# ConvGLU FFN by Strassen-Winograd on one core: two of four weight sums and the residual sums made by accumulating DMAs, the other sums moved to VectorE

## The chip, the cores and the metric

The kernel runs on one core of a Trainium2 chip. The metric is the device time of one execution in microseconds (us), taken as the median of several runs. A core has a matrix engine (PE, with PEld for its weight loads), VectorE (DVE), ScalarE (ACT), GpSimd (POOL) and SyncE (SP). SP issues the plain DMAs in order, POOL issues the DMAs that its own queue carries, and every engine works through its own instructions in the order in which the program has them.

## The reference

One layer: `x += W_out [GDN | FoX | RG-LRU](norm(x))`, then `x += ConvGLU(norm(x))`, then a final RMSNorm, for 512 prompt tokens and 8 streams of 16 tokens (640 tokens together), model width 2048, FFN width 5632, all in float32. The part that the change touches is

```
def conv_ffn(h, conv_past, w_up, conv_w, w_down):
    gp, val = jnp.split(h @ w_up, 2, axis=-1)
    gc, conv_new = causal_conv(gp, conv_past, conv_w)
    return (jax.nn.silu(gc) * val) @ w_down, conv_new
```

## The kernel before, in words

Tokens lie in the free dimension, features on the 128 partitions. A float32 product is made of three float32r products: a weight is split into a high part `wh` (a cast on ACT) and a low part `wl` (a subtraction on DVE), the activations likewise, and PE adds high times high, high times low and low times high in PSUM.

The first 1.2 ms hold the input projection, the mixers and the output projection. Then comes the FFN, with Winograd's form of Strassen's scheme: a matrix product of 2 by 2 blocks (halves of K, pairs of feature tiles, halves of 320 tokens) is done with seven block products instead of eight. The weights of one step arrive as a tile `w` of four 128x128 blocks A21, A11, A12, A22 (256 KB). I call such a tile **a weight**. Four sums S1 to S4 of its blocks are needed, and the seven operands A11, A12, A22, S1 to S4 are split into `wh` and `wl`. PE runs 21 matmuls of 320 columns for one weight (line 1077), in order, into seven PSUM tiles `p`, of which there are eight.

- `wino_w` (lines 1034 to 1055) does this for a weight: SP loads `w` (line 1042); POOL makes S1, S2 and S4 (lines 1047, 1049, 1052), DVE S3 (1048); ACT casts twice (1050 for three blocks, 1053 for four), DVE subtracts twice (1051 and 1054). `w` has 4 buffers, `wh` and `wl` 3 each. `next_w` (1057) keeps three weights ahead.
- `wino_x` (1009 to 1032) makes the seven operands of a pair of activation tiles: four subtractions on POOL (1013 to 1016), three casts on ACT, three subtractions on DVE (1025, 1028, 1031).
- `up(f)` (1331) is one up **pass**: 8 weights, then the combination of the seven products into a gate tile and a value tile (lines 1346 to 1353: one copy on ACT, nine operations on DVE), a multiplication by `corr` on POOL (1354), the convolution (line 257, twice on DVE), silu on ACT (1358), a second multiplication by `corr` on POOL (1359), four products on DVE (1362, 1366), and a store of the result to DRAM (`hT`, 1367) that POOL issues. There are 44 passes, 352 weights.
- `down(i)` (1396) is one down pass: 2 to 8 weights for one of eight pairs of output tiles. It loads the residual tiles from DRAM (`x2`, line 1402, SP), adds the seven products to them (1412, 1418, 1419 on DVE; 1415 on POOL), and stores them (1430, SP). Each pair is visited four times, 32 passes and 168 weights, the first eight passes 2, 3, 3, 4, 5, 6, 7 and 8 weights long. `form` (1377) prepares the operands of the next steps between two weights.
- `plain` (1442) and `finish` (1469) do the last step without Strassen's scheme and the final norm.

The code is written as generators, and a scheduling layer decides how the instructions stand on each engine; the sums and splits of later weights are interleaved with the work that follows a pass.

Of the kernel before, what the change touches and what calls it, by code (L numbers as in the profile page):

```python
# [35 lines left out]
def blk(t, b):  # L36
    """Token block b of a tile in halves order: 4 prompt blocks, then the samples."""
    if b < 4:
        c = (b // 2) * HALF + (b % 2) * 128
        return t[:, c:c + 128]  # L40
    return t.rearrange("p (a c) -> p a c", a=2)[:, :, 256:320]


def cblk(t, b):
    """Token block b of a tile in conv order (prompt, then per stream 3 columns apart)."""
    if b < 4:
        return t[:, 128 * b:128 * b + 128]
    return t[:, 515:667].rearrange("p (s c) -> p s c", c=19)[:, :, :16]


class K:
    def __init__(self, ctx, tc, a, cfg):
# [18 lines left out]
        # the activation tables load beside the first transfers  # L71
# [33 lines left out]
    def rsqrt(self, x, scale, eps, n, out=None):  # L105
        """(x * scale + eps) ** -0.5 to float32's accuracy."""
# [65 lines left out]
    def ahead(self, n):  # L172
        """the next pieces' two parts, up to n of them"""
# [6 lines left out]
    def split_act(self, x, g, hi, lo):  # L180
        """hi + lo = x * g exactly, for each k tile."""
# [17 lines left out]
    def bcast_tok(self, r, name):  # L199
        """r [128 tokens, 5] -> [128, 640]: r's columns one after the other, on each partition."""  # L200
# [12 lines left out]
    def evac(self, out, ps, scale=None):  # L213
        """halves order"""
# [8 lines left out]
    def evac_nat(self, out, ps, np_=P):  # L223
        """prompt tokens in order, then the samples' tokens"""
# [23 lines left out]
    def conv(self, out, x, w, width, bias=None):  # L248
        """out[c] = sum_j w[j] x[c + j] (+ bias)"""
# [11 lines left out]
    def load_x(self):  # L261
        """x * g in two parts; and the sums of x squared; yields k tile by k tile"""
# [7 lines left out]
        # the first two feature tiles' weights between the tiles of x: the second one's at half the pace  # L270
# [11 lines left out]
        # the sums of squares run behind: the odd tiles' on Pool, the even ones' on ACT and DVE  # L282
# [26 lines left out]
    def gates(self, ps):  # L309
        """softplus-based gates of GDN and FoX, their running sums, in the forms that the mixers use"""  # L310
# [16 lines left out]
        # softplus(z), token-major: z (16 columns per token block), -lambda of the LRU (4 columns)  # L327
# [44 lines left out]
        # the caches' log forget values: their sums  # L372
# [15 lines left out]
        # chunk sums of the GDN gates, running sums of the FoX ones  # L388
# [7 lines left out]
        # token-major: beta and G of the heads  # L396
# [8 lines left out]
        # exp(G), -beta exp(G), beta / 2  # L405
# [6 lines left out]
        # G of the last token of its chunk, for each token  # L412
# [11 lines left out]
        # the FoX sums as three bfloat16 parts  # L424
# [17 lines left out]
    def parts3(self, outs, x, tmp):  # L442
        """outs: three bfloat16 parts whose sum is -x"""
# [8 lines left out]
    def gdn_in(self, h, f0):  # L452
        """projections and convolutions of head h: 2 silu(.) of q, k, v, and of z"""
# [31 lines left out]
    def gdn(self, h, y, zs):  # L485
# [6 lines left out]
        # token-major, normalised, and back  # L492
# [22 lines left out]
        # decays  # L515
# [33 lines left out]
        # M, then A^T  # L549
# [19 lines left out]
        # (I + M)^-1 by doubling blocks: X the inverse, Z its transpose  # L569
# [51 lines left out]
        # the prompt's chunks, one after the other  # L621
# [35 lines left out]
        # the samples: their 8 states, each against its 16 columns of 32  # L657
# [42 lines left out]
        # norm, gate  # L700
# [8 lines left out]
    def from_blocks(self, f, out, pt, other):  # L709
        """f on pieces of (out, blocks order pt, other), out and other in halves order"""  # L710
# [5 lines left out]
    def head_norm(self, o, scale=1.0):  # L716
        """o [128 tokens, 5 blocks, 128]: over each block's columns"""
# [17 lines left out]
    def pad32(self, x):  # L735
        """[128, 8 streams x 16] -> [128, 8, 32]: stream s at its half of 32 columns, zeros beside it"""
# [1004 lines left out]
```

## Time and profile before

| | before |
|---|---|
| median of 3 runs | 3004.94 us (3001.29 to 3005.12) |
| span of the profiled execution, first to last instruction | 3000.6 us |
| mean granted TensorE clock in it | 0.983 |
| PE busy | 2888.2 us (96%) |
| DVE busy | 2315.5 us (77%) |
| POOL busy | 1631.7 us (54%) |
| ACT busy | 1109.7 us (37%) |

The profiled execution is told by its span; its own time as a run is not told apart, but it can't be under the span, and the three runs begin 0.7 us above it. The page has, for the 40 equal slices of the span (75 us each), the busy tenths of each engine and the granted clock. A group line names source line, engine, operation and tiles, and ends with the busy time, the mean of one, and the idle time of that engine just before. Timeline rows begin with the start in us from the span's start and the duration.

### The profile page before, as it was taken

Reading aid. Unit: us, or ns where it says so; the run is one execution under the profiler, and the core shown is the slowest. Engines: PE = TensorE matmul, PEld = TensorE weight load, DVE = VectorE, ACT = ScalarE, POOL = GpSimd, SP = SyncE. Lnnn points to the kernel's source line nnn. Section 1 sums busy time; section 2 is a strip of 40 time slices with the busy share of each in tenths; the row PEclk is TensorE's granted clock in tenths of the full one; section 3 lists DMA queues with packets and bytes.
Section 4 is the critical chain, followed back from the end, with each engine's and each line's share of the span. In section 5 each row is a group of like instructions: output and inputs, shape, how many; then the busy total and the mean of one; then the engine's idle time right before and its main releaser. Section 6 shows DMA issues by size and latency. Waiting matters only on the chain. (4 is left out here: it accounts for less than half of the span.)

```text
span 3000.6 us, 54322 instructions
## 1 busy us (share of the span) xinstructions
PE 2888.2 (96%) x19927; PEld 2804.4 (93%) x19927; DVE 2315.5 (77%) x3976; ACT 1109.7 (37%) x2023; POOL 1631.7 (54%) x2367
## 2 busy tenths in 40 slices
PE   8999999999999999999999999999999789999997
PEld 7999999999999999999999999999999789999996
DVE  8746545645634537899999999999999988999888
ACT  4333323323322313444444443444444334434433
POOL 3312200310300014677777777777777988888775
PEclk9999999999999999999999999999999899999998
DMA  5123143134134745433333333333333555555443
GB/s 207 56 93 109 59 143 121 59 123 143 58 109 150 264 130 179 130 105 98 98 99 101 98 98 103 99 101 98 98 98 98 171 160 156 164 163 173 155 138 119
DMA packets 175772, 369.68 MB, mean 123 GB/s; under 512 B 20137, under 2 KB 25145, under 8 KB 175505
## 3 DMA queue, kind: packets, MB, share of 16 engines
q1 hardware_dynamic: 169088, 340.28, 36.4%
q0 software_dynamic: 6416, 25.94, 2.4%
q8 instruction: 156, 2.56, 0.4%
q14 instruction: 112, 0.91, 0.1%
HBM read 306.75 MB, written 59.39 MB: 122 GB/s over the span
## 5 line engine op out<-in xcount | busy, mean ns | idle before, releaser
L1077 PE MATMUL p<-x,wh 128*128 128x320 f32 x7280 | 1625.0, 312 | 45.0 <-DVE t L1412 31.9
L1077 PEld LDWEIGHTS p<-x,wh 128*128 128x128 f32 x7280 | 1230.5, 190 | 56.4 <-DVE t L1412 36.2
L1077 PE MATMUL p<-x,wl 128*128 128x320 f32 x3640 | 1138.9, 313 | 8.9 <-DVE wl L1054 5.2
L1077 PEld LDWEIGHTS p<-x,wl 128*128 128x128 f32 x3640 | 691.5, 190 | 19.9 <-DVE wl L1054 15.1
L1054 DVE TENSOR_TENSOR wl<-ws,wh 128x512 fp32r<-128x512 f32 x520 | 527.4, 1014 | 25.3 <-ACT wh L1053 25.2
L1051 DVE TENSOR_TENSOR wl<-w,wh 128x384 fp32r<-128x384 f32 x520 | 449.6, 865 | 73.4 <-ACT wh L1050 67.7
L1053 ACT CAST wh<-ws 128x512 fp32r<-128x512 f32 x520 | 321.6, 619 | 389.4 <-POOL ws L1052 340.1
L146 PE MATMUL d<-xh,whi 128*128 128x320 f32 x1536 | 396.8, 327 | 0.0
L1050 ACT CAST wh<-w 128x384 fp32r<-128x384 f32 x520 | 264.8, 509 | 330.0 <-issue 169.8
L1052 POOL TENSOR_TENSOR ws<-w,ws 128x128 f32<-128x128 f32 x520 | 352.7, 678 | 40.4
L146 PE MATMUL d<-xl,whi 128*128 128x320 f32 x1536 | 370.8, 310 | 0.0
L146 PE MATMUL d<-xh,wlo 128*128 128x320 f32 x1536 | 370.5, 310 | 0.0
L1047 POOL TENSOR_TENSOR ws<-w 128x128 f32<-128x128 f32 x520 | 284.1, 546 | 150.3 <-DVE wl L1054 144.0
L1049 POOL TENSOR_TENSOR ws<-ws,w 128x128 f32<-128x128 f32 x520 | 344.0, 662 | 37.5
L135 DVE TENSOR_TENSOR wlo<-raw,whi 128x512 fp32r<-128x512 f32 x230 | 175.1, 761 | 212.5 <-ACT whi L134 204.8
L134 ACT CAST whi<-raw 128x512 fp32r<-128x512 f32 x230 | 142.4, 619 | 405.9 <-PE d L146 354.1
L146 PEld LDWEIGHTS d<-xh,whi 128*128 128x128 f32 x1536 | 256.9, 190 | 9.5 <-issue 5.5
L146 PEld LDWEIGHTS d<-xl,whi 128*128 128x128 f32 x1536 | 262.6, 189 | 0.2 <-issue 0.2
L146 PEld LDWEIGHTS d<-xh,wlo 128*128 128x128 f32 x1536 | 262.7, 189 | 0.0
L1048 DVE TENSOR_TENSOR ws<-w 128x128 f32<-128x128 f32 x520 | 218.3, 426 | 13.2 <-DMA w<-in_w_down 0.7
L868 POOL COPY q<-t 128x128 f32<-128x128 f32 x24 | 12.1, 523 | 261.2 <-DVE t L220 139.8
L257 DVE SCALAR_TENSOR_TENSOR t<-t,prm,t 128x656 f32<-128x656 f32 (+1 forms) x136 | 138.4, 1017 | 6.5 <-ACT t L253 3.5
(395 smaller groups left out, 3513.5 us busy)
## 6 DMA issues: line engine op xcount, KB each, us to landing
w<-in_w_up SPq DMA_DIRECT2D x352, 256.0 KB, 2.6
raw<-in_w_in SPq DMA_DIRECT2D x196, 256.0 KB, 2.8
w<-in_w_down SPq DMA_DIRECT2D x184, 256.0 KB, 2.7
t<-x SPq DMA_DIRECT2D x74, 320.0 KB, 3.6
kc<-in_ckT SPq DMA_DIRECT2D x32, 512.0 KB, 5.0
vc<-in_cv SPq DMA_DIRECT2D x32, 512.0 KB, 5.8
x<-t SPq DMA_DIRECT2D x48, 320.0 KB, 2.2
hT<-t POOLq DMA_DIRECT2D x44, 320.0 KB, 2.5
```

The source lines that it names most:

```text
L134: nc.scalar.copy(hi[:, :n], raw[:, :n])
L135: nc.vector.tensor_sub(lo[:, :n], raw[:, :n], hi[:, :n].bitcast(F32))
L146: self.nc.tensor.matmul(ps[h][:, :HALF], wt[:, w], x[:, h * HALF:(h + 1) * HALF], start=start and i == 0, stop=stop and i == 2)
L1047: nc.gpsimd.tensor_add(s[:, 0], w[:, 0], w[:, 3])
L1048: nc.vector.tensor_sub(s[:, 2], w[:, 1], w[:, 0])
L1049: nc.gpsimd.tensor_sub(s[:, 1], s[:, 0], w[:, 1])
L1050: nc.scalar.copy(hi[:, 0:3], w[:, 1:4])
L1051: nc.vector.tensor_sub(lo[:, 0:3], w[:, 1:4], hi[:, 0:3].bitcast(F32))
L1052: nc.gpsimd.tensor_sub(s[:, 3], w[:, 2], s[:, 1])
L1053: nc.scalar.copy(hi[:, 3:7], s)
L1054: nc.vector.tensor_sub(lo[:, 3:7], s, hi[:, 3:7].bitcast(F32))
L1077: nc.tensor.matmul(ps[p], l[:, wi], r[:, xi], start=i == 0 and j == 0, stop=i == n - 1 and j == 2)
```

## The change

Only the FFN is touched (besides comments). Signs and order of the blocks are changed so that the sums come out in place:

- `w` becomes a tile of seven blocks with 6 buffers, `ws` is gone. `wino_raw` loads it with two DMAs of SP (line 1045: two blocks, 128 KB; line 1046: three blocks, 192 KB), and then a DMA of POOL (line 1047) adds a fourth block, read twice, to the two blocks that line 1045 loaded: two of the four sums. It waits for line 1045's data.
- `wino_w` makes the other two sums on DVE, one after the other in place (lines 1055 and 1056, 128x128 each), and casts all seven blocks on ACT at once (1060). `wino_lo` subtracts all seven at once on DVE (1065, 128x896). `next_raw` keeps up to five loaded weights.
- `wino_x` works on a tile of seven blocks (2 buffers instead of 3), with three subtractions on DVE (1020, one of double width, 1021, 1022) and two splits.
- `combine` is shared by up and down: one copy on ACT (1112) and seven results on DVE (nine instructions in `up`, whose gate is written in two pieces). The two multiplications by `corr` in `up` are on DVE (1386, 1391).
- `down` no longer loads the residual nor adds to it. It makes the products' sums in fresh tiles, and two DMAs of POOL (line 1445) add these to `x2` in DRAM; in the last eight passes POOL's DMAs (1443) add `x2` to the tiles in SBUF instead.
- `ns_fc` is loaded by four DMAs instead of one, and the program's space for POOL's DMA descriptors is set to 4096.

```
-        nc.sync.dma_start(w.rearrange("p a c -> p (a c)"), src)
-        nc.gpsimd.tensor_add(s[:, 0], w[:, 0], w[:, 3])
-        nc.vector.tensor_sub(s[:, 2], w[:, 1], w[:, 0])
-        nc.gpsimd.tensor_sub(s[:, 1], s[:, 0], w[:, 1])
-        nc.scalar.copy(hi[:, 0:3], w[:, 1:4])
-        nc.vector.tensor_sub(lo[:, 0:3], w[:, 1:4], hi[:, 0:3].bitcast(F32))
-        nc.gpsimd.tensor_sub(s[:, 3], w[:, 2], s[:, 1])
-        nc.scalar.copy(hi[:, 3:7], s)
-        nc.vector.tensor_sub(lo[:, 3:7], s, hi[:, 3:7].bitcast(F32))
+    def wino_raw(self, src, plain):
+        w = self.wf.tile([P, 7, P], F32, tag="w", bufs=6, name=self.name("w"))
...
+            nc.sync.dma_start(w[:, 3:5], src[:, 2:4])
+            nc.sync.dma_start(w[:, 0:3], src[:, 1:4])
+            nc.gpsimd.dma_start(w[:, 3:5], src[:, 0:1].to_broadcast([P, 2, P]), accum_op=OP.add)
+    def wino_w(self, w, plain):
...
+            nc.vector.tensor_add(w[:, 5], w[:, 3], w[:, 2])
+            nc.vector.tensor_add(w[:, 6], w[:, 0], w[:, 5])
...
+        nc.scalar.copy(hi[:, 0:n], part)
+    def wino_lo(self, part, hi, lo):
...
+        self.nc.vector.tensor_sub(lo[:, 0:n], part, hi[:, 0:n].bitcast(F32))
+    def next_raw(self):
+        while len(self.wr) <= 4:
...
-        nc.gpsimd.tensor_sub(t[:, 0], f[:, 1], f[:, 0])
-        nc.gpsimd.tensor_sub(t[:, 1], f[:, 3], t[:, 0])
-        nc.gpsimd.tensor_sub(t[:, 2], f[:, 3], f[:, 1])
-        nc.gpsimd.tensor_sub(f[:, 1], f[:, 2], t[:, 1])
+        nc.vector.tensor_tensor(f[:, 4:6], f[:, 3:4].to_broadcast([P, 2, HALF]), f[:, 1:3], op=OP.subtract)
+        nc.vector.tensor_sub(f[:, 6], f[:, 1], f[:, 5])
+        nc.vector.tensor_sub(f[:, 3], f[:, 0], f[:, 6])
...
-            nc.gpsimd.tensor_mul(x[:, 2:], x[:, 2:], corr[:, 2:])
+            nc.vector.tensor_mul(x[:, 2:], x[:, 2:], corr[:, 2:])
...
-            nc.gpsimd.tensor_mul(y[:, :656], y[:, :656], corr[:, 2:])
+            nc.vector.tensor_mul(y[:, :656], y[:, :656], corr[:, 2:])
...
+                if last:
+                    nc.gpsimd.dma_start(y[e], x2[2 * i + e], accum_op=OP.add)
+                else:
+                    nc.gpsimd.dma_start(x2[2 * i + e], y[e], accum_op=OP.add)
...
+    nc = _bacc.Bacc("TRN2", target_bir_lowering=False, num_devices=1, dynamic_dma_scratch_size=4096)
```

How the instructions stand now is decided by the scheduling layer. Three places matter. In the rows, `w` is a weight, `wh` and `wl` its parts, `ws` its sums, `p` a PSUM tile, `f` and `x` an operand before and after its split, `t` a work tile; the numbers tell tiles apart.

DVE before, the last weights of an up pass ahead of its combination:

```order
L1048 TENSOR_TENSOR ws_3220_21770<-w_3219_21769 128x128
L1051 TENSOR_TENSOR wl_3218_21738<-w_3215_21735,wh_3217_21737 128x384
L1054 TENSOR_TENSOR wl_3218_21738<-ws_3216_21736,wh_3217_21737 128x512
L1048 TENSOR_TENSOR ws_3224_21804<-w_3223_21803 128x128
L1051 TENSOR_TENSOR wl_3222_21772<-w_3219_21769,wh_3221_21771 128x384
L1054 TENSOR_TENSOR wl_3222_21772<-ws_3220_21770,wh_3221_21771 128x512
```

DVE now, at the same place (the pass ends with weight w_2996; after the last row comes its combination):

```order
L1055 TENSOR_TENSOR w_3005_21239<-w_3005_21239 128x128
L1056 TENSOR_TENSOR w_3005_21239<-w_3005_21239 128x128
L1055 TENSOR_TENSOR w_3008_21270<-w_3008_21270 128x128
L1056 TENSOR_TENSOR w_3008_21270<-w_3008_21270 128x128
L1065 TENSOR_TENSOR wl_3010_21277<-w_2996_21146,wh_3009_21276 128x896
L1055 TENSOR_TENSOR w_3011_21301<-w_3011_21301 128x128
L1056 TENSOR_TENSOR w_3011_21301<-w_3011_21301 128x128
L1065 TENSOR_TENSOR wl_3013_21308<-w_2999_21177,wh_3012_21307 128x896
L1055 TENSOR_TENSOR w_3014_21332<-w_3014_21332 128x128
L1065 TENSOR_TENSOR wl_3016_21339<-w_3002_21208,wh_3015_21338 128x896
```

The weights follow each other as w_2996, 2999, 3002, 3005, 3008, 3011, 3014. Before, a sum (1048) stands one weight ahead of the split that follows it; now the sum (1055) of w_3008 stands ahead of the split (1065) of w_2996, four weights earlier, that of w_3011 ahead of the split of w_2999, and that of w_3014 ahead of the split of w_3002. Over the passes the distance goes 4, 4, 4, 3, 2, 2, 2, 3.

POOL before, around the store of a pass's result:

```order
L1049 TENSOR_TENSOR ws_3166_21361<-ws_3166_21361,w_3165_21360 128x128
L1052 TENSOR_TENSOR ws_3166_21361<-w_3165_21360,ws_3166_21361 128x128
L1367 DMA hT_12549<-t_3145_21225 128x640
L1047 TENSOR_TENSOR ws_3170_21395<-w_3169_21394 128x128
L1049 TENSOR_TENSOR ws_3170_21395<-ws_3170_21395,w_3169_21394 128x128
```

POOL now:

```order
L1047 DMA w_2999_21177<-in_w_up 128x2x128
L1047 DMA w_3002_21208<-in_w_up 128x2x128
L1399 DMA hT_12534<-t_2988_21113 128x640
L1047 DMA w_3005_21239<-in_w_up 128x2x128
L1047 DMA w_3008_21270<-in_w_up 128x2x128
L1047 DMA w_3011_21301<-in_w_up 128x2x128
```

In place of three sums for each weight POOL has one DMA for each, and the store stands between them.

DVE before, in a down pass:

```order
L1048 TENSOR_TENSOR ws_4306_29198<-w_4305_29197 128x128
L1048 TENSOR_TENSOR ws_4310_29234<-w_4309_29233 128x128
L1025 TENSOR_TENSOR x_4304_29194<-f_4279_29057,x_4303_29193 128x640
L1051 TENSOR_TENSOR wl_4308_29200<-w_4305_29197,wh_4307_29199 128x384
L1054 TENSOR_TENSOR wl_4308_29200<-ws_4306_29198,wh_4307_29199 128x512
```

DVE now, in a down pass (weights w_3894, 3897, 3900, 3903, 3906, 3920, 3925, 3928):

```order
L1055 TENSOR_TENSOR w_3920_28180<-w_3920_28180 128x128
L1065 TENSOR_TENSOR wl_3922_28187<-w_3897_28028,wh_3921_28186 128x896
L1032 TENSOR_TENSOR x_3924_28212<-f_3909_28154,x_3923_28211 128x960
L1032 TENSOR_TENSOR x_3924_28212<-f_3909_28154,x_3923_28211 128x1280
L1065 TENSOR_TENSOR wl_3927_28221<-w_3900_28060,wh_3926_28220 128x896
L1056 TENSOR_TENSOR w_3920_28180<-w_3920_28180 128x128
L1055 TENSOR_TENSOR w_3925_28214<-w_3925_28214 128x128
L1056 TENSOR_TENSOR w_3925_28214<-w_3925_28214 128x128
L1055 TENSOR_TENSOR w_3928_28246<-w_3928_28246 128x128
L1056 TENSOR_TENSOR w_3928_28246<-w_3928_28246 128x128
L1065 TENSOR_TENSOR wl_3930_28253<-w_3903_28092,wh_3929_28252 128x896
```

Here too the sum of a weight stands ahead of the split of the weight four before it, at every second split: w_3920 ahead of w_3897, w_3928 ahead of w_3903.

More of the change, by code (lines that the diff above doesn't have):

```diff
@@ L1040, in wino_w @@
+    def wino_w(self, w, plain):
+        nc = self.nc
+        part = w[:, 0:4] if plain else w
+        if not plain:
+            nc.vector.tensor_add(w[:, 5], w[:, 3], w[:, 2])
+            nc.vector.tensor_add(w[:, 6], w[:, 0], w[:, 5])
         hi = self.wf.tile([P, 7, P], F32R, tag="wh", bufs=3, name=self.name("wh"))
         lo = self.wf.tile([P, 7, P], F32R, tag="wl", bufs=3, name=self.name("wl"))
-        nc.sync.dma_start(w.rearrange("p a c -> p (a c)"), src)
-        if plain:
-            nc.scalar.copy(hi[:, 0:4], w)
-            nc.vector.tensor_sub(lo[:, 0:4], w, hi[:, 0:4].bitcast(F32))
-            return hi, lo
@@ L1047, in wino_w @@
[L1047 to L1054 removed]
+        n = part.shape[1]
+        nc.scalar.copy(hi[:, 0:n], part)
@@ L1061, in next_w @@
                 break
-            self.wq.append(self.wino_w(*src))
+            self.wr.append(self.wino_raw(*src))
+        return self.wr.pop(0) if self.wr else None
+    def next_w(self):
+        while len(self.wq) < 3:
+            if self.wn is None:
+                raw = self.next_raw()
+                self.wn = raw and self.wino_w(*raw)
+            if self.wn is None:
+                break
+            now, raw = self.wn, self.next_raw()
+            self.wn = raw and self.wino_w(*raw)
+            self.wq.append(self.wino_lo(*now))
         return self.wq.pop(0)
@@ L1082, in wino, with combine @@
         return ps
+    def combine(self, ps, u, c11, c12, c21, c22):
+        nc = self.nc
+        u1, u2 = u
+        nc.scalar.copy(u1, ps[1])
+        nc.vector.tensor_sub(u2, ps[6], u1)
+        nc.vector.tensor_add(c21, u2, ps[7])
+        nc.vector.tensor_add(u2, u2, ps[5])
+        nc.vector.tensor_add(c22, c21, ps[5])
+        c11(u1, ps[2])
+        nc.vector.tensor_add(c21, c21, ps[4])
+        c12(ps[3], u2)
 def drive(dense, streams, rep=1):
@@ L1262, in body @@
         ns_fc = c.tile([P, NF, 9, 2], F32, name="ns_fc")
-        nc.gpsimd.dma_start(ns_fc[:, :, 1:, :], a["fc0"])
+        for f in range(0, NF, 11):
+            nc.gpsimd.dma_start(ns_fc[:, f:f + 11, 1:, :], a["fc0"][:, f:f + 11])
         k.acc = c.tile([P, 658], F32, tag="corr", name="acc2")[:, :NTOK]
@@ L1396, in down, with done @@
         def down(i, end, make):
+            def done(n):
+                pos[i] = n
+            ps = yield from k.wino(end - pos[i], hops, make, pos[i], done)
             last = end == nw
@@ L1399, in down @@
                 fin[i] = k.xt()
-            xs = [fin[i][:, e * NTOK:(e + 1) * NTOK] if last else k.t() for e in range(2)]
-            for e in range(2):
-                nc.sync.dma_start(xs[e], x2[2 * i + e])
-            def done(n):
-                pos[i] = n
-            ps = yield from k.wino(end - pos[i], hops, make, pos[i], done)
-            u = c.tile([P, 658], F32, tag="corr", name=k.name("u"))
-            u2, u3 = u[:, :HALF], u[:, HALF:NTOK]
-            x = {(e, h): xs[e][:, h * HALF:(h + 1) * HALF] for e in range(2) for h in range(2)}
-            def add(e, h, b):
-                nc.vector.tensor_add(x[e, h], x[e, h], b)
-            def gadd(e, h, b):
-                nc.gpsimd.tensor_add(x[e, h], x[e, h], b)
-            nc.scalar.copy(u2, ps[1])
-            add(0, 0, ps[1])
-            nc.vector.tensor_add(u2, u2, ps[6])
-            nc.vector.tensor_add(u3, u2, ps[7])
-            add(0, 1, ps[5])
-            add(1, 1, ps[5])
-            add(0, 0, ps[2])
-            add(1, 0, ps[4])
-            add(0, 1, ps[3])
-            gadd(1, 1, u3)
-            gadd(1, 0, u3)
-            gadd(0, 1, u2)
-            if not last:
-                for e in range(2):
-                    nc.sync.dma_start(x2[2 * i + e], xs[e])
+            y = [fin[i][:, e * NTOK:(e + 1) * NTOK] if last else k.t() for e in range(2)]
+            u = c.tile([P, 658], F32, tag="corr", name=k.name("u"))
+            part = lambda e, h: y[e][:, h * HALF:(h + 1) * HALF]
+            k.combine(ps, (u[:, :HALF], u[:, HALF:NTOK]), lambda p, q: nc.vector.tensor_add(part(0, 0), p, q),
+                      lambda p, q: nc.vector.tensor_sub(part(0, 1), p, q), part(1, 0), part(1, 1))
+            for e in range(2):
+                if last:
+                    nc.gpsimd.dma_start(y[e], x2[2 * i + e], accum_op=OP.add)
+                else:
+                    nc.gpsimd.dma_start(x2[2 * i + e], y[e], accum_op=OP.add)
         blocks = (0, 128, HALF - 128)
```

74 lines of the change are left out of this document (33 added, 41 removed).

## The prediction

> **What bounds the kernel now.** I read the page's busy times and slices first. The two slice rows are PE's busy tenths and the granted clock in tenths, 75 us a slice.
>
> ```profile
> PE 2888.2 (96%) x19927; PEld 2804.4 (93%) x19927; DVE 2315.5 (77%) x3976; ACT 1109.7 (37%) x2023; POOL 1631.7 (54%) x2367
> PE   8999999999999999999999999999999789999997
> PEclk9999999999999999999999999999999899999998
> ```
>
> PE is busy 96%, so whatever relieves another engine can win back only PE's idle time and its slow clock. Both sit in slices 32 to 34, where the up passes end and the down passes begin. Next, the windows of the middle of the up passes, of the first eight down passes, and of the other 24 (busy us and count of PE, PEld, DVE, ACT, POOL; clock; DMA share; GB/s):
>
> ```profile
> 1400.00:2300.00 900.00, 897.77 (x6068) 889.68 (x6067) 855.36 (x1408) 364.60 (x688) 692.88 (x1122) 1.00 0.34 99
> 2349.00:2505.00 156.00, 132.78 (x799) 127.90 (x798) 139.44 (x210) 59.51 (x108) 136.36 (x174) 0.91 0.54 172
> 2505.00:2936.00 431.00, 412.53 (x2728) 407.59 (x2729) 385.78 (x613) 169.48 (x317) 350.12 (x494) 0.98 0.50 156
> ```
>
> In the up passes PE has no gap, although DVE is at 95%. In the down passes it has. For the pace I take timeline rows: two PE rows three matmuls apart, the copy that opens the combination of two neighbouring up passes, of the last up pass, and of the eighth and the last down pass.
>
> ```profile
> 1805.02 0.31 PE L1077 MATMUL p<-x,wl 128*128 128x320 f32 x1
> 1805.46 0.31 PE L1077 MATMUL p<-x,wl 128*128 128x320 f32 x1
> 1788.00 0.42 ACT L1346 COPY t<-p 128x320 f32<-128x320 f32 x1
> 1812.80 0.42 ACT L1346 COPY t<-p 128x320 f32<-128x320 f32 x1
> 2349.43 0.41 ACT L1346 COPY t<-p 128x320 f32<-128x320 f32 x1
> 2505.09 0.42 ACT L1416 COPY u<-p 128x320 f32<-128x320 f32 x1
> 2937.44 0.42 ACT L1416 COPY u<-p 128x320 f32<-128x320 f32 x1 [3.81 <-POOL x L1415]
> ```
>
> Three matmuls take 0.44 us, so a weight's 21 take 3.08 us and an up pass of 8 weights 24.64. The pass takes 24.80: there is 0.16 us to win in each. The first eight down passes (38 weights) take 155.7 us against 117 of PE, the other 130 weights 432.4 against 400. So some 70 us are to be had in the down passes, hardly anything elsewhere. The waits agree:
>
> ```profile
> L1077 PE MATMUL p<-x,wh 128*128 128x320 f32 x7280 | 1625.0, 312 | 45.0 <-DVE t L1412 31.9 <-ACT wh L1050 5.1 <-DVE t L1347 3.5
> ```
>
> Of 45 us of idle time before these matmuls, 31.9 end with line 1412, the combination of a down pass.
>
> **What the change costs on DVE.** Rows of the three DVE operations for a weight (ns min/median/max):
>
> ```profile
> L1048 DVE TENSOR_TENSOR ws<-w x520: 276/433/970, 1216.4 to 2924.1; 128x128 f32<-128x128 f32 x174
> L1051 DVE TENSOR_TENSOR wl<-w,wh x520: 543/812/1760, 1226.5 to 2929.3; 128x384 fp32r<-128x384 f32 x174
> L1054 DVE TENSOR_TENSOR wl<-ws,wh x520: 676/946/2114, 1227.0 to 2930.3; 128x512 fp32r<-128x512 f32 x174
> ```
>
> The medians, beside POOL's sums, make 2.19 us a weight. The minima, which I take as undisturbed, lie on 0.143 us + 1.04 ns per column. After: two sums of 0.28 and one subtraction of 896 columns, 1.08: 1.64 us. DVE gains 0.55 us a weight; the two `corr` products cost 2 x 0.83 of it a pass (656 columns), the sums for an operand 0.81 + 2 x 0.48. POOL's sums leave. ACT stays far from full. PE's matmuls are only reordered. So DVE's time stops binding, and what is late next is the new round trip.
>
> **The round trip.** It is a wait that the change adds. Weight m+6 takes the buffer of weight m. SP's load (1045) waits for m's subtraction (1065), POOL's adding DMA (1047) for that load, the sum (1055) on DVE for the adding DMA; queued behind that sum on DVE stands whatever the order puts there. Call L the time from the end of subtraction m to the start of sum m+6. The rows that are nearest (KB each, median us to landing; then one start of POOL's DMA after DVE's release):
>
> ```profile
> prm<-in_prm SPq DMA_DIRECT2D x1, 138.0 KB, 2.2
> w<-in_w_up SPq DMA_DIRECT2D x352, 256.0 KB, 2.6
> x<-t SPq DMA_DIRECT2D x48, 320.0 KB, 2.2
> out_o_lc<-ns_lc POOLq DMA_DIRECT2D x1, 54.0 KB, 2.2
> hT<-t POOLq DMA_DIRECT2D x44, 320.0 KB, 2.5
> x<-t POOLq DMA_DIRECT2D x32, 320.0 KB, 3.1
> 1777.48 0.22 DVE L1366 TENSOR_TENSOR t<-t,t 128x64 f32<-128x64 f32 x1
> 1777.99 0.58 POOL L1367 DMA_DIRECT2D hT<-t  x1 [0.85 <-DVE t L1366]
> ```
>
> SP's 128 KB: 2.2. POOL starts 0.29 after its release. An adding DMA of POOL isn't in this trace. A store of 128 KB by POOL would land in about 2.3 (between 2.2 and 2.5); loads take longer than stores (SP: 2.6 for 256 KB against 2.2 for 320), about 0.5, so 2.8; 0.1 for reading the destination gives 2.9. Lower bound 2.3 (no dearer than the store), upper 3.6 (the 3.1 row plus the 0.5). With 0.05 for the wakes L = 2.2 + 0.3 + 2.9 + 0.05 = 5.45, from 4.85 to 6.15.
>
> By the Trainium skill (DMA: Bandwidth & Descriptors, Anatomy of one DMA) a DMA of this queue takes 2.0 us plus its bytes at 436 GB/s, an estimate of 2.3 for 128 KB, which would make L 4.85 and the change faster; the traced 320 KB store, 2.5 against the 2.75 of that rule, is no slower than it, but no row here shows the rule for a load that adds.
>
> **Up passes.** In the changed order sum n+4 stands ahead of the subtraction of n (the pass's last weight), and sum n+6 ahead of that of n+2, after which the combination follows. So subtraction n can't end before subtraction n-2 + L + 0.28 + 0.28 + 1.08, and n+2 not before n + L + 0.28 + 1.08. From n+2 to n+6, which is the next pass's n-2, DVE has the rest of the pass. Its rows:
>
> ```profile
> 1789.13 0.47 DVE L1347 TENSOR_TENSOR t<-t,p 128x320 f32<-128x320 f32 x1
> 1789.53 0.37 DVE L1048 TENSOR_TENSOR ws<-w 128x128 f32<-128x128 f32 x1
> 1792.40 0.55 DVE L1051 TENSOR_TENSOR wl<-w,wh 128x384 fp32r<-128x384 f32 x1
> 1795.32 0.98 DVE L257 SCALAR_TENSOR_TENSOR t<-t,prm,t 128x656 f32<-128x656 f32 x1
> 1796.22 0.81 DVE L1051 TENSOR_TENSOR wl<-w,wh 128x384 fp32r<-128x384 f32 x1
> 1777.15 0.41 DVE L1362 TENSOR_TENSOR t<-t,t 128x256 f32<-128x256 f32 x1
> 1777.62 0.68 DVE L1054 TENSOR_TENSOR wl<-ws,wh 128x512 fp32r<-128x512 f32 x1
> ```
>
> Starts overlap ends by some 0.07, so I count from start to start. Combination 3.0 (1789.13 to 1792.40 less a sum of 0.29), two convolution steps of 0.9, two products by `corr` of 0.75, the four final products 0.95, four subtractions of 1.0, four sums of 0.2: 12.1. The cycle is 2L + 3.0 + 12.1, less the overlaps, about 2L + 15.0. At L = 5.45 that is 25.9 us instead of 24.80, and PE waits for the combination to free its PSUM tiles: 43 x 1.1 = **+47 us**. The cycle hides under PE's 24.64 only up to L = 4.82.
>
> **Down passes.** Every second subtraction stands behind a sum four weights on, so two weights take L + 1.5 (one or two sums and a subtraction); the combination falls into the wait. 130 weights x 6.95/2 = 452 against 432: **+20**. In the first eight passes the distance is smaller and DVE's own work counts: 38 x 1.64 + 8 x 3.0 + nine operands of 4.4 (sums, and 1.14 + 1.48 for the splits) + 5 left of the last up pass = 131 against 155.7: **-25**; the waits for POOL's sums and for line 1415 go with it. Residual loads, adds and stores give way to two adding DMAs a pass: issued in 2 x 0.58 between the weights' DMAs, they delay one link in three, perhaps: 24 x 0.39 = **+9**, between 0 and 28. In the last pass they land under the 14 us that `plain` takes to reach that pair (8 x 12 matmuls x 0.147). Operands' sums beside the output projection, the four loads of `ns_fc`, SP's second issue: nothing, under PE's work.
>
> Sum: 47 + 20 - 25 + 9 = +51. The span, 3000.6, lies 4.3 us under the median, so I add the difference to the median: **3056 us**. 0.2%, 6 us, is about what a measurement of this kernel can tell from no change. The sum is zero at L = 5.1, that is a landing of 2.55.
>
> **Rivals.**
>
> *The adding DMA is as quick as a store* (2.3, L = 4.85). Up passes at 24.7: -4; 130 weights at 6.35/2: -19; first passes -25: **2957 us**. It decides from a landing below 2.55. For it: POOL's small stores land in 2.2. Against: every load row is dearer than the store beside it. 0.33.
>
> *Descriptors are held up.* If DVE's work kept POOL from writing them, or their space of 4096 were too small, each adding DMA would land up to one DVE subtraction later, 1.08: L = 6.5, up 43 x 3.2 = +138, down 520 - 432 = +88, +9 - 25: **3215 us**.
>
> ```profile
> L1367 POOL DMA_DIRECT2D hT<-t x44: 581/581/590, 1282.4 to 2369.6; - x44
> ```
>
> Against it: POOL's issue takes 581 to 590 ns each time, beside a DVE at 95%. 0.10. The Trainium skill (SBUF — State Buffer, SBUF: two separate sides) says that GpSimd can't write descriptors while DVE runs a two-port operation; by that rule this rival would come true for such operations, and the trace's even 581 ns shows none here.
>
> **Numbers.** Forecast 0.52 (above +6 us); a landing near 2.55, no difference, 0.05; so faster 0.33, same 0.05, slower 0.62. Range: from 2950, just under the quick rival (with 130 weights at PE's pace it is 2944), to a landing of 3.6: L = 6.15, +108 + 65 + 9 - 25 = +157, 3162, so 3165. The held-up rival is left out. The forecast's own range is 3011 to 3165.
>
> **What would show it.** Right: copies of neighbouring up passes 25.9 apart, DVE idle ahead of line 1055 until line 1047's DMA lands, that landing at 2.9, subtractions (1065) near 1.08, PE idle behind the combination. Wrong: 24.7 between the copies and landings below 2.5 (quick), or POOL's issues well over 0.6 us (held up). If landings are at 2.9 and the passes still at 24.7, the cycle itself is misread.

## The result, and the profile after

The changed kernel takes 3359.28 us (median of 4 runs, 3351.96 to 3364.8) against 3005.03 before: ratio 1.1179, 95% interval 1.1162 to 1.1196. It is slower, as forecast, but by 354 us where 51 were forecast, and outside the range. The profiled execution has a span of 3350.2, 349.6 more than before's.

The page of the changed kernel, busy times and the two slice rows of PE:

```profile
PE 2999.2 (90%) x19927; PEld 2900.0 (87%) x19927; DVE 2020.2 (60%) x4090; ACT 1055.9 (32%) x1474; POOL 987.5 (29%) x1094
...
PE   8999999999999988898888988888888888777877
...
PEclk9999999999999999999989999999899999898988
```

DVE and POOL were relieved as forecast (2315.5 to 2020.2, 1631.7 to 987.5), and yet PE, which had 96%, has idle time from the first up pass to the last down pass. The windows of the up passes, of the first eight down passes and of the other 24 (busy us and count of PE, PEld, DVE, ACT, POOL; clock; DMA share; GB/s):

```profile
1268.00:2557.00 1289.00, 1139.21 (x7208) 1118.19 (x7209) 828.01 (x1765) 406.33 (x479) 471.12 (x561) 0.94 0.62 135
2557.00:2705.00 148.00, 127.12 (x803) 122.57 (x802) 116.32 (x224) 56.29 (x64) 59.62 (x55) 0.94 0.88 193
2705.00:3285.00 580.00, 462.05 (x2733) 448.20 (x2733) 313.97 (x605) 155.61 (x178) 193.44 (x172) 0.89 0.68 140
```

No engine is full in any of them; the kernel is now a chain of waits. PE's busy time rose too, by 111 us, at a lower granted clock (0.948 on average, 0.983 before); the first experiment below brings both back (2863.5 us, 0.989) with the same instructions, so the clock is taken here as following from the waits. The copies that open the combinations (up, then down: count, ns min/median/max, first and last start), and the copy of the eighth down pass:

```profile
L1112 ACT COPY t<-p x44: 412/419/429, 1268.2 to 2557.9; 128x320 f32<-128x320 f32 x44
L1112 ACT COPY u<-p x32: 413/427/430, 2573.2 to 3285.4; 128x320 f32<-128x320 f32 x32
```

```profile
2705.47 0.42 ACT L1112 COPY u<-p 128x320 f32<-128x320 f32 x1
```

43 up passes take 1289.7 us, 29.99 each, and before (same rows of that trace, 1267.0 to 2349.4) 1082.5. So the 349.6 us divide into +207.2 in the up passes, 147.6 against 155.7 (-8.1) in the first eight down passes, 580.0 against 432.4 (+147.6) in the other 24, and +2.9 before and behind.

ACT has the longest waits (1150.3 us, until PE frees its `wh`). Of DVE's and POOL's, the longest are those of the predicted round trip; PE's wait for the combination stands below them (total, times, longest):

```profile
DVE w L1055 <- DMA w<-in_w_up: 418.5, 199, 6.3
POOL w L1047 <- DMA w<-in_w_up: 407.6, 183, 6.9
DVE w L1055 <- DMA w<-in_w_down: 280.2, 103, 7.0
PE p L1101 <- DVE t L1113: 150.9, 44, 5.5
```

One link of it in the timeline, from the subtraction of a weight to the sum of the weight that takes its buffer:

```profile
1801.59 1.09 DVE L1065 TENSOR_TENSOR wl<-w,wh 128x896 fp32r<-128x896 f32 x1
...
1802.70 0.33 SPq L1045 DMA_DIRECT2D w<-in_w_up  x1
...
1805.68 1.19 POOL L1047 DMA_DIRECT2D w<-in_w_up  x1 [4.48 <-DVE wl L1065]
...
1808.24 1.18 POOL L1047 DMA_DIRECT2D w<-in_w_up  x1 [1.37 <-DMA w<-in_w_up]
...
1809.76 0.29 DVE L1055 TENSOR_TENSOR w<-w 128x128 f32<-128x128 f32 x1 [4.70 <-DMA w<-in_w_up]
...
1810.30 1.08 DVE L1065 TENSOR_TENSOR wl<-w,wh 128x896 fp32r<-128x896 f32 x1
1811.30 0.48 DVE L1113 TENSOR_TENSOR t<-p,t 128x320 f32<-128x320 f32 x1
...
1811.84 0.77 PE L1101 MATMUL p<-x,wh 128*128 128x320 f32 x2 [4.34 <-DVE t L1113]
...
1814.21 1.09 DVE L1065 TENSOR_TENSOR wl<-w,wh 128x896 fp32r<-128x896 f32 x1
1814.23 1.19 POOL L1047 DMA_DIRECT2D w<-in_w_up  x1 [4.57 <-DVE t L1118]
```

The buffer is free at 1802.67. SP's load goes out at once and lands at 1804.85; POOL issues the adding DMA 2.98 us after the load went out (the row of 1805.68; it names DVE, which had long been done), and the sum starts another 4.08 later: L is 7.1 here. DVE has stood idle for 4.70 us by then, the combination (1113) starts at 1811.30, and PE, which needs it for its PSUM tiles, has stood for 4.34. The DMAs (KB each, median us from issue to landing), and the times that POOL is busy with issuing (1047 and 1445 add, 1399 stores; the last row is the landing of 1445):

```profile
w<-in_w_up SPq DMA_DIRECT2D x352, 128.0 KB, 2.3
w<-in_w_up POOLq DMA_DIRECT2D x352, 128.0 KB, 3.7
```

```profile
L1047 POOL DMA_DIRECT2D w<-in_w_up x352: 1174/1188/1677, 1208.1 to 2536.1; - x176
...
L1399 POOL DMA_DIRECT2D hT<-t x44: 592/592/619, 1287.3 to 2574.7; - x44
...
L1445 POOL DMA_DIRECT2D x<-t x48: 918/1430/1976, 2577.5 to 3156.4; - x48
...
DMA to landing us min/median/max: 4.4/7.6/9.9
```

An adding DMA of 128 KB lands in 3.7 us where 2.9 (2.3 to 3.6) was taken, and keeps POOL for 1.19 where a store of 320 KB takes 0.59. Over all sums that start within 0.06 us of their DMA's landing (209 of 341 between the first and the last opening copy of the up passes), L has a median of 7.47.

### The profile page after: what moved, and what is told of

It is laid out like the page before. It is cut to its first block, busy times and chain, and to the rows that moved or that the text cites. A ratio compares the mean times of both kernels' runs of the same rounds, so it can differ in the third digit from the quotient of the medians.

```text
span 3350.2 us, 53510 instructions
## 1 busy us (share of the span) xinstructions
PE 2999.2 (90%) x19927; PEld 2900.0 (87%) x19927; DVE 2020.2 (60%) x4090; ACT 1055.9 (32%) x1474; POOL 987.5 (29%) x1094
## 5 line engine op out<-in xcount | busy, mean ns | idle before, releaser
L1101 PE MATMUL p<-x,wh 128*128 128x320 f32 x7280 | 1713.4, 325 | 248.8 <-DVE t L1113 150.9
L1101 PEld LDWEIGHTS p<-x,wh 128*128 128x128 f32 x7280 | 1296.2, 201 | 280.3 <-DVE t L1113 162.5
L1060 ACT CAST wh<-w 128x896 fp32r<-128x896 f32 (+1 forms) x536 | 501.3, 936 | 1365.2 <-PE p L1101 1150.3
L1101 PEld LDWEIGHTS p<-x,wl 128*128 128x128 f32 x3640 | 727.9, 200 | 55.8 <-DVE wl L1065 55.7
L1047 POOL DMA_DIRECT2D w<-in_w_up x352 | 419.4, 1196 | 759.2 <-DMA w<-in_w_up 407.6
L1065 DVE TENSOR_TENSOR wl<-w,wh 128x896 fp32r<-128x896 f32 (+1 forms) x536 | 579.2, 1081 | 64.5 <-ACT wh L1060 63.1
L1055 DVE TENSOR_TENSOR w<-w 128x128 f32<-128x128 f32 x520 | 150.6, 291 | 699.8 <-DMA w<-in_w_up 418.5
L1047 POOL DMA_DIRECT2D w<-in_w_down x168 | 203.8, 1216 | 462.3 <-DMA w<-in_w_down 208.8
L1056 DVE TENSOR_TENSOR w<-w 128x128 f32<-128x128 f32 x520 | 145.9, 289 | 7.8
L1030 ACT CAST x<-f 128x960 fp32r<-128x960 f32 (+1 forms) x58 | 63.7, 1126 | 43.5 <-DVE f L1022 28.1
L1032 DVE TENSOR_TENSOR x<-f,x 128x960 fp32r<-128x960 f32 (+1 forms) x58 | 75.8, 1322 | 0.4 <-ACT x L1030 0.2
```

Of the source, the lines that this page charges most:

```text
L1030: nc.scalar.copy(h3[:, a:b], f[:, a:b])
L1032: nc.vector.tensor_sub(l3[:, a:b], f[:, a:b], h3[:, a:b].bitcast(F32))
L1047: nc.gpsimd.dma_start(w[:, 3:5], src[:, 0:1].to_broadcast([P, 2, P]), accum_op=OP.add)
L1055: nc.vector.tensor_add(w[:, 5], w[:, 3], w[:, 2])
L1056: nc.vector.tensor_add(w[:, 6], w[:, 0], w[:, 5])
L1060: nc.scalar.copy(hi[:, 0:n], part)
```

## The experiments

All times of passes are worked out like those above, from the opening copies. Up passes: mean of 43. The medians of the kernel before, run again beside each group of experiments, lie between 3002.55 and 3005.03 us, and each ratio is taken to the one beside it.

| kernel | median us | ratio to before (95%) | up pass | first 8 down | other 24 |
|---|---|---|---|---|---|
| before | 3005.03 | | 25.17 | 155.7 | 432.4 |
| changed | 3359.28 | 1.118 (1.116 to 1.120) | 29.99 | 147.6 | 580.0 |
| sums at most 1 ahead | 2941.02 | 0.980 (0.978 to 0.981) | 24.62 | 130.4 | 422.1 |
| at most 2 ahead | 2966.12 | 0.987 (0.986 to 0.989) | 24.63 | 135.6 | 440.2 |
| at most 3 ahead | 3043.70 | 1.013 (1.011 to 1.015) | 24.69 | 144.9 | 505.6 |
| adding, 128 pieces | 3276.67 | 1.091 (1.089 to 1.093) | 28.87 | 143.7 | 557.1 |
| copying, 256 pieces | 3175.03 | 1.058 (1.056 to 1.059) | 27.26 | 141.4 | 530.0 |
| copying, 128 pieces | 3142.10 | 1.045 (1.044 to 1.047) | 27.07 | 132.8 | 520.3 |
| residual by loads and stores | 3263.78 | 1.087 (1.085 to 1.090) | 30.11 | 142.0 | 502.8 |
| residual left out | 3307.36 | 1.100 (1.097 to 1.104) | 30.06 | 137.8 | 545.0 |
| POOL adds in SBUF | 2989.23 | 0.995 (0.993 to 0.996) | 24.64 | 138.6 | 459.7 |
| 1 ahead, residual by loads and stores | 2952.66 | 0.983 (0.981 to 0.984) | 24.62 | 136.8 | 428.2 |
| 1 ahead, POOL adds | 2930.85 | 0.976 (0.974 to 0.977) | 24.71 | 131.1 | 406.7 |
| 1 ahead, both | 2949.21 | 0.982 (0.980 to 0.983) | 24.71 | 137.7 | 419.5 |

### Is it the place of the sums on DVE?

```
-            nc.vector.tensor_add(w[:, 5], w[:, 3], w[:, 2])
+            s = nc.vector.tensor_add(w[:, 5], w[:, 3], w[:, 2])
+            if len(self.subs) >= 1:
+                self.tc.add_manual_dep(s.ins, self.subs[-1].ins.name, mybir.DependencyInfo(
+                    mybir.DependencyClass.NoSync, mybir.DependencyReason.DATA), reason="order")
...
-        self.nc.vector.tensor_sub(lo[:, 0:n], part, hi[:, 0:n].bitcast(F32))
+        self.subs.append(self.nc.vector.tensor_sub(lo[:, 0:n], part, hi[:, 0:n].bitcast(F32)))
...
```

> The changed kernel, with one thing more: on VectorE the sum (1055) of weight m+2 must stand behind the subtraction (1065) of weight m, so that no sum is more than one weight ahead of the split that follows it. Instructions, DMAs and buffers stay the same. Theory (a cycle through the six buffers: subtraction of weight m, load, adding DMA, sum of weight m+6, which stands on VectorE ahead of the subtraction of weight m+2): with L as traced, 7.5 us, the order gives 2L + 15.0 = 30.0 us a pass; with the sums one weight ahead L has five weights, 15 us, to pass, and the cycle is gone. Up passes back to 24.7 to 25.0 us, median 2950 to 3030 us. Rival (supply: POOL's queue can't bring the adding DMAs faster, since it waits for each weight's load in turn): the order changes nothing, 30 us a pass, 3340 to 3370 us. Rival (clock: what is lost is mostly TensorE at a lower clock after short gaps): in between, 3100 to 3300 us.

2941.02 us, 9 under the expected range, and the up passes at PE's own pace (24.62). Its page and its opening copies:

```profile
PE 2863.5 (97%) x19927; PEld 2793.0 (95%) x19927; DVE 2005.9 (68%) x4090; ACT 1049.6 (36%) x1474; POOL 1031.1 (35%) x1094
...
PEclk9999999999999999999999999999999999999998
...
w<-in_w_up POOLq DMA_DIRECT2D x352, 128.0 KB, 4.0
```

```profile
L1115 ACT COPY t<-p x44: 421/422/428, 1265.7 to 2324.4; 128x320 f32<-128x320 f32 x44
L1115 ACT COPY u<-p x32: 413/420/428, 2334.5 to 2876.9; 128x320 f32<-128x320 f32 x32
```

The adding DMAs are no quicker (4.0 us), but they land a median 6.2 us before the up passes' sums want them. 418 us go by a change of order alone: the DMAs keep their length and are no longer waited for. The rivals of supply and of clock fall.

### How far ahead may a sum stand?

The same edge, with `self.subs[-3]` and with `self.subs[-2]`.

> The changed kernel with the sum (1055) of weight m+4 kept behind the subtraction (1065) of weight m on VectorE, so that a sum is at most three weights ahead. Theory (cycle): in the order that results, the longest chain of a pass goes through two waits for L, five other VectorE steps and two splits: 2L + 3.3 + 5.75 (combination 3.0, two subtractions, one product), which at L = 7.0 to 7.5 is 23.1 to 24.1 us, just hidden under 24.64. Down: three weights need L + 1.65, 8.7 to 9.7 at the down passes' longer L, against 9.24. Up passes 24.64 to 25.0, median 2941 to 2995 us, all of the rest in the down passes. Rival (the loss grows evenly with the distance of the sums): two thirds of the way from one weight ahead to four, over 3150 us.

> The changed kernel with the sum (1055) of weight m+3 kept behind the subtraction (1065) of weight m, so that a sum is at most two weights ahead. Theory: four weights, 12.3 us of TensorE, have to cover L + 1.65, which is 9.1 to 10.7 at L of 7.5 to 9.0: hidden. Up passes 24.6 to 24.7, last 24 down passes 415 to 435 us, median 2935 to 2960 us, as with one weight ahead. Rival (the loss grows with the distance, one weight 2941, three 3044 us): 2975 to 3010 us.

In the up passes both came out as the cycle has it: 24.69 and 24.63, hidden at three ahead, not at four (29.99). In the down passes both cost more than expected. At three ahead:

```profile
L1115 ACT COPY t<-p x44: 412/418/429, 1264.1 to 2325.6; 128x320 f32<-128x320 f32 x44
L1115 ACT COPY u<-p x32: 409/420/428, 2341.6 to 2976.0; 128x320 f32<-128x320 f32 x32
```

505.6 us for the last 24 passes, where three weights in L + 1.65, at that run's L of 8.75 (median of the 70 sums that wait), give 130/3 x 10.4 = 451. The trace divides the other 55: over all 126 sums of these passes L is 9.45 on average (30 us more), and from the start of a sum to the end of the subtraction behind it pass 2.20 us, not 1.65 (24 us more). So DVE's other work there does not fall wholly into the wait. At two ahead the waits that are left are of the same kind (99.9 us of DVE for the down weights' DMA between 2460 and 2890), with L at 11 us in these passes. The totals, 3043.70 and 2966.12, lie 49 and 6 us over their expected ranges; neither rival fits (over 3150, and 2975 to 3010).

### What makes the landing long?

```
-            nc.gpsimd.dma_start(w[:, 3:5], src[:, 0:1].to_broadcast([P, 2, P]), accum_op=OP.add)
+            nc.gpsimd.dma_start(w[:, 3:5], src[:, 0:2], accum_op=OP.add)
```

> The changed kernel with an adding DMA that reads two neighbouring blocks (1024 bytes in one piece for each partition) in place of one block twice (two pieces of 512 bytes); so the two sums have a wrong summand, and it moves as many bytes into SBUF. Theory A (POOL's issue of 1.19 us, and with it the landing, goes with the number of pieces, 256): 128 pieces make the issue 0.6 to 0.9 us and the landing 3.1 to 3.4 us; L falls by 0.3 to 0.6 us, which is twice in each of 43 up passes and once in each two of 130 down weights, 45 to 90 us: 3270 to 3315 us. Theory B (adding itself makes the issue and the landing long, whatever the pieces): issue 1.19, landing 3.7, 3345 to 3370 us.

The second kernel only drops `accum_op=OP.add`, the third does both. The two sums are wrong or left out in all three, so these kernels tell times alone.

> The changed kernel with POOL's DMA (1047) copying the block twice into place instead of adding it: it leaves the two sums out, in the same shape and order and with the same waits. Theory A (pieces): the issue stays at 1.1 to 1.2 us and the landing falls little, by 0 to 0.3 us: 3310 to 3360 us. Theory B (adding): issue near 0.6 and landing 2.3 to 2.8 us, so L falls by about 1.1 us and the time by 43 x 2 x 1.1 + 65 x 1.1 = 166 us: 3180 to 3220 us.

> The changed kernel whose DMA of POOL (1047) copies, instead of adding, and reads two neighbouring blocks, 1024 bytes in one piece for each partition; it leaves the two sums out. It completes the square of adding or copying, 256 or 128 pieces, of which three corners stand (issue on POOL 1.19, 0.85 and 0.71 us; landing 3.71, 3.24 and 2.87). Theory A (adding costs a fixed time for each piece, so that half the pieces halve it): issue 0.55 to 0.65 us, landing 2.5 to 2.7. Theory B (adding costs a fixed time for each DMA, pieces another): issue 0.35 to 0.45, landing 2.3 to 2.5. The cycle 2L + 15.0 with L of 5.5 to 5.9: up passes 26.0 to 26.8 us, total 3080 to 3135 us. Rival (something other than L sets the pace of the up passes): as with the copy in 256 pieces, 27.3.

Issue and landing, adding in 128 pieces:

```profile
L1047 POOL DMA_DIRECT2D w<-in_w_up x352: 845/852/1149, 1206.3 to 2485.2; - x176
...
w<-in_w_up POOLq DMA_DIRECT2D x352, 128.0 KB, 3.3
```

Copying in 256 pieces:

```profile
L1047 POOL DMA_DIRECT2D w<-in_w_up x352: 702/714/742, 1208.2 to 2414.4; - x176
...
w<-in_w_up POOLq DMA_DIRECT2D x352, 128.0 KB, 2.9
```

Copying in 128 pieces:

```profile
L1047 POOL DMA_DIRECT2D w<-in_w_up x352: 537/537/553, 1207.4 to 2408.0; - x176
...
w<-in_w_up POOLq DMA_DIRECT2D x352, 128.0 KB, 2.6
```

Both theories have a part: the copy in 256 pieces lies between them in issue (0.71), lands in 2.9, later than B had it, and takes 3175.03 us, 5 under B's range. A further 128 pieces cost 0.18 us of issue when copying (2.6 to 2.9 to landing), 0.34 when adding (3.3 to 3.7). Adding costs 0.32 of issue with 128 pieces and 0.47 with 256, and 0.62 and 0.84 to landing (medians 2.64 to 3.25, and 2.87 to 3.71). With the pieces change their size (1024 or 512 bytes) and their source (two blocks once, or one block twice); which of these counts is not shown. The last run's issue came near theory A (0.55 to 0.65). The pace of the up passes follows L, taken in each run as above:

| | L | 2L + 15.0 | up pass |
|---|---|---|---|
| adding, 256 pieces | 7.47 | 29.9 | 29.99 |
| adding, 128 | 6.89 | 28.8 | 28.87 |
| copying, 256 | 6.21 | 27.4 | 27.26 |
| copying, 128 | 6.13 | 27.3 | 27.07 |

The last run stands 0.3 us over its expected 26.8 (and 7 over in total) because L fell by less than the landing did; by itself it does not tell the theory from its rival, the four together do. The sum is good to about 0.5 us: in the two runs on the residual further down, whose up passes are those of the changed kernel, L is 7.30 and 7.24, which gives 29.6 and 29.5 for the 30.11 and 30.06 measured.

### Without an adding DMA for the weights

```
-            nc.sync.dma_start(w[:, 3:5], src[:, 2:4])
-            nc.sync.dma_start(w[:, 0:3], src[:, 1:4])
-            nc.gpsimd.dma_start(w[:, 3:5], src[:, 0:1].to_broadcast([P, 2, P]), accum_op=OP.add)
+            nc.sync.dma_start(w[:, 3:6], src[:, 1:4])
+            nc.sync.dma_start(w[:, 0:3], src[:, 0:3])
+            nc.gpsimd.tensor_tensor(w[:, 3:5], w[:, 3:5], w[:, 5:6].to_broadcast([P, 2, P]), op=OP.add)
...
```

The order of the blocks in DRAM, and the blocks that `plain` picks, change with it.

> The changed kernel without its adding DMAs for the weights: the block that they added comes with SP's second load (192 KB each now), and GpSimd adds it in SBUF to the other two with one instruction of 128x256. VectorE's order is left to the scheduler; sums stand 2 to 5 weights ahead of the split that follows, no less than in the changed kernel. The residual sums still use adding DMAs. Theory (cycle through the buffers, 2L + 15.0 in the up passes): L is a load of 2.4 to 2.9, a wake of 0.1 to 0.3, an addition of 0.5 to 1.0, so 3.2 to 4.2 us, the cycle 21.4 to 23.4 us, hidden under TensorE's 24.64; two down weights need L + 1.5, up to 5.7, under 6.16. Up passes 24.64 to 24.75, median 2930 to 2975 us. Rival (the order by itself, with its distant sums, costs the time, whatever brings the blocks): over 3200 us.

```profile
L1047 POOL TENSOR_TENSOR w<-w x520: 722/833/4370, 1207.9 to 2899.4; 128x256 f32<-128x256 f32 x174
...
w<-in_w_up SPq DMA_DIRECT2D x704, 192.0 KB, 2.5
w<-in_w_down SPq DMA_DIRECT2D x336, 192.0 KB, 3.2
```

Sums no less far ahead than in the changed kernel, and up passes of 24.64: a distant sum costs nothing there, where the round trip is short (L has a median of 5.10 over all sums of the up passes). The time is 14 us over the expected 2975, all in the last 24 passes (459.7): there loads take 3.2 us, not 2.5, and two weights in L + 1.5 are hidden only up to L = 4.66. The rival (over 3200) falls.

### The residual's accumulating DMAs

```
+            xs = [k.t() for _ in range(2)]
+            for e in range(2):
+                nc.sync.dma_start(xs[e], x2[2 * i + e])
...
-                    nc.gpsimd.dma_start(y[e], x2[2 * i + e], accum_op=OP.add)
...
-                    nc.gpsimd.dma_start(x2[2 * i + e], y[e], accum_op=OP.add)
+                nc.vector.tensor_add(y[e], y[e], xs[e])
+                if not last:
+                    nc.sync.dma_start(x2[2 * i + e], y[e])
```

> The changed kernel with the residual sums of the down passes made as loads (SP), additions (VectorE, two of 640 columns a pass) and stores (SP), in place of the accumulating DMAs of POOL. Theory (these DMAs, 1.43 us of issue each and two in a pass, stand between the weights' adding DMAs on POOL's queue and lengthen every third link of the down cycle): 20 to 70 us less, 3290 to 3340 us, all of it in the down passes, up passes unchanged at 30 us. Rival (they are hidden, the weights' cycle is late anyway): 3350 to 3370 us.

That run fell by more (3263.78), but the scheduler had also brought the down passes' sums nearer, to 2 to 4 ahead, so it does not say what the DMAs cost. The next one leaves the order as it was and drops both DMAs:

> The changed kernel without the accumulating DMAs of the residual: it leaves the residual sum and the sums of a pair's four visits out. VectorE's order stays as in the changed kernel, sums three to four weights ahead in the last 24 down passes, where putting back loads, additions and stores had also moved the sums nearer (2 to 4). Theory (in the last 24 down passes two weights take L + 1.5; the residual's DMAs cost only what they add to L): 130/2 links shorter by 0.2 to 0.6 us, 13 to 39 us, so these passes fall from 580 to 541 to 567 us, and the time to 3315 to 3350 us; what putting back the loads brought above that came with the nearer sums. Rival (the residual's DMAs themselves cost the 77 us of these passes): 495 to 515 us for these passes, 3260 to 3285 us.

```profile
L1112 ACT COPY t<-p x44: 412/419/430, 1266.3 to 2558.7; 128x320 f32<-128x320 f32 x44
L1112 ACT COPY u<-p x32: 411/424/430, 2576.9 to 3241.5; 128x320 f32<-128x320 f32 x32
```

545.0 us in the last 24 passes, 35 less than with the DMAs, and 9.8 less in the first eight: the theory's figure (541 to 567), not the rival's (495 to 515). The total, 3307.36, lies 8 us under the expected range. Of the 77 us that the run before had won in the last 24 passes, about 42 are left for the nearer sums.

How these DMAs lengthen L can be read from the changed kernel. Of the 126 sums of the last 24 passes, 58 had their load (1045) in flight together with a residual DMA: these loads landed in 4.12 us (median), the other 68 in 2.13. From the load's landing to POOL's issue it is 0.69 and 0.68. So the residual's DMAs did not make POOL's issues late; the loads beside them landed later. In the run without these DMAs the median is 2.21.

With the cycle gone the same DMAs are a gain:

> The kernel with the sums one weight ahead, and with the residual sums of the down passes as loads, additions on VectorE and stores again. In the changed kernel this was worth 95 us, since each residual DMA lengthened a link of the buffers' cycle. Theory: with the cycle gone they stand beside TensorE's work, and only what is left idle in the down passes, 20 us (552 us for 532 of TensorE), can change: 2930 to 2945 us. Rival (they cost DMA time by themselves, whatever the cycle: DMA engines 93 to 98% busy in these passes): 2900 to 2925 us.

2952.66, 12 us slower than with accumulating DMAs, and 8 over the expected 2945; the rival (2900 to 2925) is further off. Why they are a gain here was not varied further.

### Versions that beat both

> No adding DMAs at all: weights' sums by one GpSimd addition, residual sums on VectorE with loads and stores, sums one weight ahead on VectorE. Theory: up passes at TensorE's 24.64, down passes at 168 x 3.08 = 517 plus what the first eight passes and the combinations cost, 525 to 550: 2915 to 2942 us. Rival (GpSimd's additions slow VectorE's by sharing SBUF, as its three sums did before): subtractions over 1.2 us, no better than 2942 us.

> Sums one weight ahead on VectorE, the weights' block added by GpSimd in SBUF instead of by a DMA, the residual still by accumulating DMAs. Theory (with the cycle gone it does not matter who adds the weights' block; the residual's DMAs spare VectorE and SP work in the down passes): 2930 to 2945 us, level with the adding DMAs (2941). Rival (adding DMAs load the DMA engines, 93 to 98% busy in the down passes, and that costs time): 2915 to 2930 us.

2949.21 and 2930.85. The first ("1 ahead, both" in the table) lies 7 us over its expected range; the subtractions take 1.15 us on average there, over the 1.08 of the kernel with sums one ahead, under the rival's 1.2, so neither text fits it. The second is the fastest of all, 2.4% under before: sums one ahead, POOL's one addition for the weights, accumulating DMAs for the residual. It is 10 us under the kernel with sums one ahead (2941.02): 15 less in the last 24 passes and 4 more in the up passes. A window of 410 us over those passes in both, the one with adding DMAs first:

```profile
2460.00:2870.00 410.00, 398.18 (x2651) 391.65 (x2650) 297.33 (x581) 149.97 (x172) 188.59 (x168) 0.99 0.93 192
```

```profile
2460.00:2870.00 410.00, 407.52 (x2755) 403.70 (x2754) 350.77 (x614) 154.53 (x180) 158.88 (x174) 1.00 0.67 179
```

The DMA engines are 93% busy in the one and 67% in the other, for 192 and 179 GB/s, and PE has 12 and 2 us of idle time. 2930.85 lies at the edge between the theory (2930 to 2945) and the rival (2915 to 2930). The lower load on the DMA engines goes with the gain; that it is the cause is not shown, since POOL's issues go as well.

## Why the prediction was right and wrong

**What bounds the kernel.** That PE's idle time and its slow clock were all there was to win held: the sums one ahead bring the up passes to 24.62 us, PE's own 24.64. But besides 0.16 us a pass there were 16 us more in the up passes: their mean was 25.17, not 24.80, mostly since the last pass, with the operands for down, took 36.4. I read the pace off two neighbours.

**DVE's costs, POOL's relief.** Right: subtractions 1.08, sums 0.29 (the row of 1809.76), DVE at 60% of the span.

**The round trip.** The mechanism was right in each step, in place and in form: the sum four weights ahead, the wait on line 1047, PE behind the combination, two links in a pass. The step that failed is the size of L. Predicted: 2.2 + 0.3 + 2.9 + 0.05 = 5.45, at most 6.15. Measured medians: 2.34 for SP's load, 0.68 from its landing to POOL's issue, 3.71 to the landing, 0.05 for the other two: 6.78, and 7.47 on the 209 links that count, where the load takes 2.70 and the adding DMA 3.98 on average. Most of the miss is in the landing, and there in the 0.1 that the sum had for reading the destination: no run shows that term, and adding cost 0.62 and 0.84. I priced an adding DMA by rows of stores, whose issue is half as long, and the wake by a row that waits for DVE (0.29), not for a DMA. The four kernels of the table above show that two things lengthen the landing, adding and the read in 256 pieces of 512 bytes, and that even a copy in 256 pieces lands in 2.9, which I had allowed for the whole.

**Up passes.** 2L + 15.0 is 29.9 at the measured L, and 29.99 was measured. +47 became +207: the longer L adds 43 x 2 x 2.02 = 174, and the misread pace of before takes 16 away, together 205.

**Down passes.** Two weights in L + 1.5, with L at the median of that stretch (7.96), make 615 us against 580 measured; the other four runs with that order lie within 6% of the same sum (545 to 558 for 520 to 557), but it does not follow their differences. +20 became +148 with the residual's part. That part, 9 us with 28 as a bound, was 45 (35 and 10), and by another path than predicted. The accumulating store does keep POOL for 1.43 us, not 0.58, and lands in 7.6; but POOL's issues for the weights came no later by it, while the loads in flight beside it took 4.12 us, not 2.13. The first eight passes: -25 was predicted, -8 came. That sum counted DVE's work and no round trip, and 15 of 39 sums there start at their DMA's landing. With the sums one ahead these passes take 130.4, where 131 was forecast; in part that is luck, since DVE is busy for 115 us of them and the DMA engines all the time (a share of 1.00).

**The rivals.** The quick landing (2.3) did not come. Its 2957 also left out the +9 of the residual that the other sums have; with it, it is 2966. By the Trainium skill (DMA: Bandwidth & Descriptors, Anatomy of one DMA) 128 KB take an estimated 2.3 us; the copy in 128 pieces takes 2.6 here, the adding DMA 3.7. The same section of the Trainium skill calls descriptor generation "small, variable"; one issue keeps POOL busy for 0.54 to 1.19 us here. The held-up rival came nearest in size (L = 6.5, 3215 us), not in cause: POOL's issue is as long (1.19, 1.18) while DVE stands idle, from 1805.1 to 1809.8 in the timeline above, as beside the subtraction of 1814.21 (1.19). The Trainium skill's rule (SBUF — State Buffer, SBUF: two separate sides), that GpSimd can't write descriptors while DVE runs a two-port operation, does not show in those rows; whether the subtraction is such an operation, no row tells. The descriptors' space of 4096 was not varied; two adding DMAs stood back to back in 2.44 us in the trace (from 1819.39), without a wait between.

**The order.** That sums stand four ahead was read from the order, and it decides the outcome as much as L does. I took it as given and asked only what L would be; I did not ask what the change is worth with another order. Sums one ahead are worth 418 us.

## What to carry to other kernels

A DMA that sits in a buffer's round trip is paid for by the in-order engine that waits for it, and what it costs depends on the distance at which its user stands in that engine's queue as much as on the round trip's length: here shorter DMAs won up to 217 us, a nearer place for the sums 418. Look first for a waiting instruction that stands ahead of work it does not need, and put it behind. Where the pace is a cycle of k round trips, bound their length by a DMA of the same kind and the same number of pieces; if no row has one, let the range of the time be as wide as k times that doubt. An adding DMA saves engine work, but it has a price in issue and landing that grows with the pieces. Here it paid for the residual (12 us, with the sums one ahead), and not for the weights, where one addition by POOL was 10 us faster.

## What the runs showed of the hardware

- POOL's issue of a DMA of 128 KB: 0.54 us (copying, 128 pieces of 1024 bytes), 0.71 (copying, 256 of 512), 0.85 and 1.19 (adding, the same two). DVE does not matter to it: with DVE idle and with DVE busy all through the issue, the medians are 537 and 537, 714 and 712, 850 and 854, 1188 and 1197 ns.
- POOL starts a DMA 0.62 to 0.68 us after the landing it waits for (medians of the four kernels), but an addition 0.12 to 0.16 us after (the middle half, in the kernel in which POOL adds in SBUF). What the difference is stays open.
- An accumulating store of 320 KB to DRAM lands in 7.6 us (median), a plain one by POOL in 3.4 in the up passes of the same run (line 1399), and plain stores of the residual by SP in 3.4 in the down passes of the run that has them.
- In the last 24 down passes of the changed kernel, SP's loads of 128 KB landed in 4.12 us (median) when an accumulating residual DMA was in flight beside them, and in 2.13 when none was; in the run without these DMAs it was 2.21.
